# Three value projections join gate columns in pairs that use Strassen's products

## The chip, the cores and the metric

The kernel runs on one core of a Trainium2 chip. The metric is the device time of one execution in microseconds (us). Before the change it is 1405.8 us, the median of three runs from 1404.01 to 1406.87 us. The engines are named as in the profile: PE multiplies matrices, DVE and ACT work on whole tiles, POOL and SP here mostly issue transfers. Each engine runs its own list of instructions in a fixed order.

## The reference

One decoder layer on 256 tokens of width 2048, all in float32. Cut to what matters here:

```python
h = rmsnorm(x, g_mix)
proj = h @ w_in                                   # 2048 x (3*2048 + 3*2048)
q, k, v = first 3*2048 columns, 16 heads of 128 each
gates = sigmoid(the last 3*2048 columns)          # three branches
o_a = stick_breaking_attention(q[:4], k[:4], v[:4])
qn, kn = rmsnorm(q[4:]) * q_gain, rmsnorm(k[4:]) * k_gain
o_b, o_c = moba_attention(6 heads), dilated_attention(6 heads)   # softmax with biases
x = x + (sum over branches of gates * (o @ w_branch)) @ w_out
x = x + (silu(h2 @ w_g) * (h2 @ w_u)) @ w_down,   h2 = rmsnorm(x)
```

The change is in `proj` alone, 24 blocks of 512 columns: four each for q, k and v (a block is one group of four heads) and twelve for the gates (four column blocks of three branches).

## The kernel before, in words

**Precision.** Every float32 product is made of three: a weight tile (128 rows of K by two, 512 columns) is split by `split` (L110) into a high part, an ACT cast into `w_hi`, and a low part, a DVE subtraction into `w_lo`. `product` (L174 to L178) then does high by high, low by high, high by low, each a matmul of 128x512. `w_hi` and `w_lo` have five buffers each, so splits run at most five tiles ahead of PE.

**Plain blocks.** `project` multiplies one block of 512 columns over all of K: 8 splits and 16 x 2 x 3 = 96 matmuls (16 slices of K, two halves of the tokens).

**Pairs.** `project_pair` takes two blocks of columns at once. Half of K (chunks 0 and 1, `WC`) goes by Strassen's seven products: 7 x 2 x 2 x 3 = 84 matmuls in place of 96. The other half goes plainly: 96. A pair has 22 splits and 180 matmuls where two plain blocks have 16 and 192. It also forms sums of weight tiles on DVE (`add_into`, L320, six of 128x1024; L331 in `begin_pair`, two), copies three intermediate results on ACT (`snapshot`, L315) and combines results on DVE (L375, L377, L380, L389). In the order of the code, PE does: first product (weights b11), second (b21), fifth (sum `u`), two plain slices, sixth (`u`), a plain slice, seventh (`b12` + `b22`), a plain slice, third (b22), two plain slices, fourth (`u`), two plain slices. Each of these steps is twelve matmuls. ACT copies the first product right after it, and the fifth, sixth and seventh right after each of them.

**Stages.** Small generators run beside the projections. `parts` and `project` call `advance(stages)` at each split or slice and `advance(slow_stages)` at every second one. After a q and k pair of group g, `rows_to_columns` normalises and transposes q and k of that group: 16 sums of squares on ACT (L663, of 128x128), the root by Ln and Exp with two table loads (L185, L186) and eight small DVE steps (L189 to L192), a scaling on DVE for each of four tiles (L681), and then, for groups 0 to 2, transposes on PE (L198), copied out by DVE for q (L691) and by ACT for k (L688). Transposed tiles go through the PSUM pool `tr`, which has two buffers. For group 3 the transposes are made by DMA: ACT copies (L650), issues the transpose (L652), and eight splits later `join` copies the landed words (L673, ACT); q is then scaled on DVE (L676). `attention` of group g follows in `slow_stages` once `keep_v` has stored the values of the group, which needs the attention of the group before to be written out. Group 0 (stick-breaking) uses Ln and Exp on ACT and steps of 128x768 on DVE; groups 1 to 3 use softmax.

**Order.** A scheduler sets the order of instructions within an engine, except for those that `keep_in_program_order` pins. `add_into`, the DMA transposes and `join`'s copies are pinned. The order of the projection's units is the list `units`: v0, one gate block, qk0, qk1, v1, qk2, v2, qk3, v3, one gate block, and then five pairs of gate blocks. At the second of the five pairs the attention PSUM is given back, and the pairs use two further PSUM banks from then on (`beside`); before that all four banks of a pair come from `acc` (`in_turn`). From the same place the finished attention outputs are split for the next stage (`split_o`, four splits of 128x1024, one in each of the last four pairs).

Of the kernel before, what the change touches and what calls it, by code (L numbers as in the profile page):

```python
# [29 lines left out]
NB = 512  # L30
# [27 lines left out]
def hybrid_block(ctx: ExitStack, tc: tile.TileContext, x, w_in, w_branch, w_out, w_gu, w_down, rel_bias, xT, gains,  # L58
# [3 lines left out]
    w_in, w_branch, w_out, w_gu, w_down = (w[0] for w in (w_in, w_branch, w_out, w_gu, w_down))  # L62
# [20 lines left out]
    def pool(stack, name, side, bufs=1):  # L83
        return stack.enter_context(tc.tile_pool(name=name, bufs=bufs, side=side, reuse_waits="tile"))
# [8 lines left out]
    def half_kb(dt=F32):  # L93

        return scratch.tile([P, NB], dt, name="sc")
# [13 lines left out]
    def split(hi, lo, src, pin=False):  # L109
        for op in nc.scalar.copy(hi, src), nc.vector.tensor_sub(lo, src, hi.bitcast(F32)):  # L110
            if pin:
                tc.keep_in_program_order(op)
# [6 lines left out]
    split_count = [0]  # L119
    at_split = {}  # L120
# [31 lines left out]
    def finish_stages(queue):  # L152
        while queue:
            advance(queue)

    def project(acts, k0, w, row0, nk, col0, ps=None, done=0, last=1):


        ps = ps or banks()
        held = []  # L160
        for k, w_hi, w_lo in weights(w, row0, done, nk, col0):
            if k:
                advance(stages)
            if k % 2 == 0 and k:
                advance(slow_stages)
            held.append((k, w_hi, w_lo))
            if k < nk - last or k == nk - 1:
                for t in range(NT):
                    for kk, hi, lo in held:
                        product(ps[t], *acts.plain(t, k0 + kk), hi, lo, kk == 0, kk == nk - 1)  # L170
                held = []
        return ps
# [152 lines left out]
    def begin_pair(acts, w, colA, colB):  # L325

        b11, b12 = (quarter(acts, w, 0, col0) for col0 in (colA, colB))
        p11 = [parts(b) for b in b11]
        u = [gx.tile([P, 2, NB], F32, name="u") for _ in acts.wc]
        for a, b, d in zip(b11, b12, u):  # L330
            nc.vector.tensor_add(d, a, b)  # L331
        b21 = quarter(acts, w, 1, colA)
        return p11, b12, u, b21, [parts(b) for b in b21]
# [69 lines left out]
    hs = Both(p1, h, WC)  # L403
# [21 lines left out]
    V0 = 2 * NH * HD  # L425
# [43 lines left out]
    def first_norm():  # L469
        rows = []  # L470
        for c in range(4):
            rows.append(load_x(c, fetch))
            yield
            if c:
                squares(rows[c - 1], ss1, c - 1)
            yield
        squares(rows[3], ss1, 3)
        yield
        sst = small.tile([P, NT], F32, name="sst", bufs=1)
        nc.vector.tensor_reduce(sst, ss1, op=ALU.add, axis=AX.X)  # L480
        rsqrt_mean(rstd, sst, D, NT)
        yield
# [219 lines left out]
    def until_joined(g):  # L702
        while len(joined) < 4 * (g + 1):
            yield

    def attention(g, qT, kT, v):
        biases = []
        if g:
            for hl in (0, 2):
                bias = pa.tile([P, 2, S], F32, name="bias")  # L710
                nc.sync.dma_start(bias, bass.AP(tensor=vec.tensor, offset=vec.offset + (4 * g - H_A + hl) * NDIST,
                                                  ap=[[1, P], [NDIST, 2], [1, S]]))
                biases.append(bias)
        for hl in (0, 2):
            if g:
                yield from softmax_pair(4 * g + hl, hl, qT, kT, v, biases[hl // 2])
            else:
                yield from stick_breaking(hl, qT, kT, v)
            yield
# [3 lines left out]
    def keep_gate(c, b, srcs):  # L723
        for t in range(NT):
            gt = half_kb()
            nc.scalar.activation(gt, srcs[t], AF.Sigmoid, scale=rstd[:, t:t + 1])
            nc.gpsimd.dma_start(gate_mem[b, c, t], gt)
# [3 lines left out]
    def keep_v(g, ps):  # L731
        if g:
            finish_stages(slow_stages)
        heads["v", g] = v = pa.tile([P, NT, NB], F32, name="v", bufs=1)

        def scaled():
            for t in range(NT):
                nc.scalar.activation(v[:, t, :], ps[t], AF.Copy, scale=rstd[:, t:t + 1])
            yield

        if g:
            finish_stages([scaled()])
            slow_stages.append(until_joined(g))
            slow_stages.append(attention(g, *heads["qk", g], v))
        else:
            stages.extend((first_norm(), scaled()))

    def keep_qk(g, q0, q1, k0, k1):
        sbs = []
        if not g:  # L750
            q_scale = small.tile([P, NT], F32, name="sst", bufs=1)
            nc.vector.tensor_scalar(q_scale, rstd, SCALE, None, op0=ALU.mult)
        for t, (src, own) in enumerate(((q0, True), (q1, False), (k0, True), (k1, True))):
            sb = src if own else half_kb()
            nc.scalar.activation(sb, src, AF.Copy, scale=(rstd if g or t >= NT else q_scale)[:, t % NT:t % NT + 1])
            sbs.append(sb)
        heads["qk", g] = qkT = [pa.tile([P, 4, S], F32, name=f"{n}T") for n in "qk"]
        if g:
            stages.append(rows_to_columns(g, sbs, qkT))
        else:  # L760
            slow_stages.append(rows_to_columns(g, sbs, qkT))
            slow_stages.append(attention(g, *qkT, heads["v", g]))
# [1 line left out]


    chunks = [(c, b) for c in range(4) for b in range(3)]
    units = [("v", 0), ("gate", chunks[0]), ("qk", 0), ("qk", 1), ("v", 1), ("qk", 2), ("v", 2), ("qk", 3), ("v", 3)]
    units += [("gate", chunks[1])] + [("gates", chunks[i:i + 2]) for i in range(2, len(chunks), 2)]

    def gate_col(c, b):  # L770
        return 3 * NH * HD + b * D + c * NB

    def pair_of(kind, what):
        if kind == "qk":
            return hs, w_in, what * NB, NH * HD + what * NB
        if kind == "gates":
            return hs, w_in, gate_col(*what[0]), gate_col(*what[1])

    def in_turn():
        turn.reverse()  # L780
        return [acc.tile([P, NB], F32, name=turn[1]) for _ in range(2)]
# [4 lines left out]
    def split_o(k):  # L786
        split(o.hi[:, k:k + 4, :], o.lo[:, k:k + 4, :], o_raw[:, k:k + 4, :], True)
# [1 line left out]
    others = in_turn  # L789
    ahead = None  # L790
    for (kind, what), after in zip(units, units[1:] + [(None, None)]):
        if kind == "gates" and what[0] == chunks[4]:
            finish_stages(slow_stages)
            pat.close()
            acc2 = ctx.enter_context(tc.tile_pool(name="acc2", bufs=1, space=PSUM))
            others = beside
            o = Columns(pool(ph1, "o", "left"), "o", NH)
            for i in range(NH // 4):
                at_split[split_count[0] + 22 * i + 12] = [lambda k=4 * i: split_o(k)]
        nxt = pair_of(*after)  # L800
        if kind in ("qk", "gates"):
            ps, ahead = project_pair(*pair_of(kind, what), ahead, nxt)
            if others is in_turn:
                turn.reverse()
        else:
            ps = project(h, 0, w_in, 0, KT, V0 + what * NB if kind == "v" else gate_col(*what),
                         *((ps0, FIRST) if (kind, what) == ("v", 0) else ()))
            ahead = begin_pair(*nxt) if nxt else None
        finish_stages(stages)
        if kind == "v":  # L810
            keep_v(what, ps)
        elif kind == "qk":
            keep_qk(what, *ps)
        elif kind == "gate":
            keep_gate(*what, ps)
        else:
            keep_gate(*what[0], ps[:2])
            keep_gate(*what[1], ps[2:])
# [22 lines left out]
    for c in range(4):  # L841
        turning = [rooms[(NT * c + t) % len(rooms)] for t in range(NT)]
        ms = [room[:, :NB] for room in turning]
        for b, (k0, nk) in enumerate(((0, H_A), (H_A, H_B), (H_A + H_B, H_C))):
# [3 lines left out]
            ps = project(o, k0, w_branch, k0 * P, nk, c * NB)  # L848
# [49 lines left out]
    for c in range(4):  # L898
# [3 lines left out]
        ps = project(m, 0, w_out, 0, KT, c * NB)  # L902
# [250 lines left out]
```

## Time and profile before

| | |
|---|---|
| timed runs, median of 3 | 1405.8 us (1404.01 to 1406.87) |
| profiled execution, from first to last instruction | 1402.7 us |
| PE busy | 1394.4 us (99%) |
| DVE busy | 1208.7 us (86%) |
| ACT busy | 959.1 us (68%) |
| POOL busy | 20.1 us |
| HBM traffic over the span | 220 GB/s |
| granted PE clock, mean | 1.000 |

The profiled execution's own time is not listed beside its span; the median of the timed runs is 3.1 us longer than the span. A matmul record shows 0.39 us, but matmuls overlap: their starts stand about 0.2265 us apart, which is what one costs. In a list of groups the last numbers are busy time, the mean of one, and the idle time of the engine just before. In a table by stretch, the columns are us, then for each engine busy time and instructions in brackets, granted clock, DMA share and GB/s.

The stretches of the projection, read from where the results of each unit are taken: v0 and a gate block to 51 us, qk0 to 92, qk1 to 140, v1 to 170, qk2 to 213, v2 to 246, qk3 to 286, v3 to 313, a gate block to 331, and the pairs of gate blocks to 378, 420, 461, 502 and 544 us.

### The profile page before, as it was taken

What the parts mean: (1) busy time and instruction counts of PE and PEld (TensorE: products, weight loads), DVE (VectorE), ACT (ScalarE), POOL (GpSimd) and SP (SyncE); (2) the same over time, 40 slices, a digit from 0 to 9 for tenths busy, and PEclk for the clock granted to TensorE, in tenths of its full rate; (3) what the DMA queues carried; (4) which work ended last, traced back from release to release, by engine and by line L of the source; (5) the groups of instructions that cost most, each with busy time, mean ns of one, the idle gap of its engine ahead of it and who ended that gap; (6) DMA issues with size and microseconds to landing.
All of it is one profiled execution on the core that took longest, in us unless ns stands there. A gap on an engine that the chain in (4) does not pass through costs nothing. (4 is left out here: it accounts for less than half of the span.)

```text
span 1402.7 us, 17407 instructions
## 1 busy us (share of the span) xinstructions
PE 1394.4 (99%) x6197; PEld 1150.2 (82%) x6197; DVE 1208.7 (86%) x1290; ACT 959.1 (68%) x1204; POOL 20.1 (1%) x45
## 2 busy tenths in 40 slices
PE   9999999999999999999999999999999999999998
PEld 7888888888888888888878888888888888788887
DVE  6997887857899997875789999999999998997887
ACT  7777867787767675666767677776776776754553
POOL 1000000000000000000000000000000000000000
PEclk9999999999999999999999999999999999999999
DMA  9764647684657667998876766677877779877562
GB/s 341 277 225 125 235 123 251 182 228 137 235 202 246 223 200 264 326 278 243 263 232 239 225 205 222 205 210 250 250 234 240 231 226 307 281 239 260 196 198 87
DMA packets 208967, 320.56 MB, mean 229 GB/s; under 512 B 53064, under 2 KB 65376, under 8 KB 208880
## 3 DMA queue, kind: packets, MB, share of 16 engines
q1 hardware_dynamic: 153216, 293.64, 62.8%
q10 hardware_dynamic: 53136, 17.86, 6.6%
q0 software_dynamic: 2528, 7.95, 1.5%
q8 instruction: 48, 0.79, 0.2%
q14 instruction: 39, 0.32, 0.1%
HBM read 294.22 MB, written 14.70 MB: 220 GB/s over the span
## 5 line engine op out<-in xcount | busy, mean ns | idle before, releaser
L110 DVE TENSOR_TENSOR w_lo<-w_raw,w_hi 128x1024 fp32r<-128x1024 f32 x324 | 393.0, 1220 | 96.9 <-ACT w_hi L110 95.3
L110 ACT CAST w_hi<-w_raw 128x1024 fp32r<-128x1024 f32 x324 | 337.2, 1050 | 107.1 <-PE qs L178 29.5
L110 ACT CAST w_hi<-g_raw 128x1024 fp32r<-128x1024 f32 x192 | 199.8, 1052 | 110.4 <-PE ps L178 38.1
L110 ACT CAST w_hi<-u 128x1024 fp32r<-128x1024 f32 x144 | 151.5, 1053 | 150.2 <-DVE u L320 75.5
L110 DVE TENSOR_TENSOR w_lo<-g_raw,w_hi 128x1024 fp32r<-128x1024 f32 x192 | 228.8, 1220 | 25.4 <-ACT w_hi L110 24.3
L110 DVE TENSOR_TENSOR w_lo<-u,w_hi 128x1024 fp32r<-128x1024 f32 x144 | 172.2, 1220 | 19.0 <-ACT w_hi L110 13.7
L177 PE MATMUL ps<-w_lo,h_hi 128*128 128x512 f32 x352 | 137.5, 391 | 0.0
L178 PE MATMUL ps<-w_hi,h_lo 128*128 128x512 f32 x352 | 137.3, 390 | 0.0
L176 PE MATMUL ps<-w_hi,h_hi 128*128 128x512 f32 x352 | 131.2, 390 | 0.0
L177 PE MATMUL qs<-w_lo,h_hi 128*128 128x512 f32 x332 | 129.8, 391 | 0.0
L178 PE MATMUL qs<-w_hi,h_lo 128*128 128x512 f32 x332 | 129.3, 390 | 0.0
L176 PE MATMUL qs<-w_hi,h_hi 128*128 128x512 f32 x332 | 124.6, 394 | 0.0
L320 DVE TENSOR_TENSOR u<-u,g_raw 128x1024 f32<-128x1024 f32 x80 | 94.4, 1219 | 0.0
L177 PEld LDWEIGHTS ps<-w_lo,h_hi 128*128 128x128 f32 x352 | 66.1, 188 | 13.8
L178 PEld LDWEIGHTS ps<-w_hi,h_lo 128*128 128x128 f32 x352 | 66.1, 188 | 13.6
L176 PEld LDWEIGHTS ps<-w_hi,h_hi 128*128 128x128 f32 x352 | 65.9, 188 | 13.6
L178 PEld LDWEIGHTS qs<-w_hi,h_lo 128*128 128x128 f32 x332 | 62.3, 188 | 13.0
L176 PEld LDWEIGHTS qs<-w_hi,h_hi 128*128 128x128 f32 x332 | 62.3, 188 | 12.8 <-issue 0.2
L177 PEld LDWEIGHTS qs<-w_lo,h_hi 128*128 128x128 f32 x332 | 62.4, 188 | 12.7
L331 DVE TENSOR_TENSOR u<-g_raw 128x1024 f32<-128x1024 f32 x40 | 48.7, 1219 | 10.7 <-DMA g_raw<-in_w_in 9.5
L320 DVE TENSOR_TENSOR g_raw<-g_raw 128x1024 f32<-128x1024 f32 x40 | 47.1, 1218 | 0.0
L177 PE MATMUL v<-w_lo,h_hi 128*128 128x512 f32 x120 | 46.9, 390 | 0.0
(400 smaller groups left out, 2933.1 us busy)
## 6 DMA issues: line engine op xcount, KB each, us to landing
w_raw<-in_w_in SPq DMA_DIRECT2D x116, 512.0 KB, 4.8
g_raw<-in_w_gu SPq DMA_DIRECT2D x88, 512.0 KB, 5.5
w_raw<-in_w_gu SPq DMA_DIRECT2D x88, 512.0 KB, 5.9
g_raw<-in_w_in SPq DMA_DIRECT2D x72, 512.0 KB, 5.7
w_raw<-in_w_down SPq DMA_DIRECT2D x56, 512.0 KB, 5.3
w_raw<-in_w_branch SPq DMA_DIRECT2D x32, 512.0 KB, 5.9
w_raw<-in_w_out SPq DMA_DIRECT2D x32, 512.0 KB, 4.7
g_raw<-in_w_down SPq DMA_DIRECT2D x32, 512.0 KB, 5.3
```

The source lines that it names most:

```text
L110: for op in nc.scalar.copy(hi, src), nc.vector.tensor_sub(lo, src, hi.bitcast(F32)):
L176: nc.tensor.matmul(ps, ah, wh, start=start, stop=False, **how)
L177: nc.tensor.matmul(ps, ah, wl, start=False, stop=False, **how)
L178: nc.tensor.matmul(ps, al, wh, start=False, stop=stop, **how)
L320: tc.keep_in_program_order(nc.vector.tensor_add(d, d, a))
L331: nc.vector.tensor_add(d, a, b)
```

## The change

The plain blocks v1, v2, v3 and the second gate block, and one of the pairs of gate blocks, are regrouped: each of v1, v2, v3 is now made in a pair with one gate block (`vg`). The units become v0, a gate block, qk0, qk1, vg1, qk2, vg2, qk3, vg3, and four pairs of gate blocks. Of 24 blocks, 22 are now in eleven pairs (18 in nine before). The first results of a `vg` pair go to `keep_v`, the second to `keep_gate`. The attention PSUM is now given back at the last but one pair of gates (`LAST_HEADS = 2`), so attention 3 has two pairs of gates to run beside, and `split_o` is called every eleven splits in the last two pairs and at the start of the next stage.

```diff
-    units = [("v", 0), ("gate", chunks[0]), ("qk", 0), ("qk", 1), ("v", 1), ("qk", 2), ("v", 2), ("qk", 3), ("v", 3)]
-    units += [("gate", chunks[1])] + [("gates", chunks[i:i + 2]) for i in range(2, len(chunks), 2)]
+    units = [("v", 0), ("gate", chunks[0]), ("qk", 0), ("qk", 1)]
+    for g in range(1, 4):
+        units += [("qk", g)] * (g > 1) + [("vg", (g, chunks[g]))]
+    units += [("gates", chunks[i:i + 2]) for i in range(4, len(chunks), 2)]
+    LAST_HEADS = 2
...
+        if kind == "vg":
+            return hs, w_in, V0 + what[0] * NB, gate_col(*what[1])
...
-        if kind == "gates" and what[0] == chunks[4]:
+        if kind == "gates" and what[0] == chunks[4 + 2 * LAST_HEADS]:
...
-                at_split[split_count[0] + 22 * i + 12] = [lambda k=4 * i: split_o(k)]
+                at_split[split_count[0] + 11 * i + 8] = [lambda k=4 * i: split_o(k)]
...
-        if kind in ("qk", "gates"):
+        if kind in ("qk", "gates", "vg"):
             ps, ahead = project_pair(*pair_of(kind, what), ahead, nxt)
...
+        elif kind == "vg":
+            keep_v(what[0], ps[:2])
+            keep_gate(*what[1], ps[2:])
```

The scheduler makes a new order of it. Three places matter below; in each, rows of the same step stand before and after. The first is DVE while q and k of group 2 are normalised, beside v2 before:

```order
L192 TENSOR_TENSOR rr<-rs_y_2003,rs_t_2006 128x16
L110 TENSOR_TENSOR w_lo<-g_raw,w_hi 128x1024
L681 TENSOR_TENSOR sc<-sc,rr 128x512 x4
L110 TENSOR_TENSOR w_lo<-g_raw,w_hi 128x1024
L110 TENSOR_TENSOR w_lo<-u,w_hi 128x1024
L691 TENSOR_TENSOR qT<-tr,gq 128x4x128
L110 TENSOR_TENSOR w_lo<-u,w_hi 128x1024
```

The same step beside vg2, on DVE in the changed kernel:

```order
L192 TENSOR_TENSOR rr<-rs_y_2272,rs_t_2275 128x16
L681 TENSOR_TENSOR sc<-sc,rr 128x512 x2
L320 TENSOR_TENSOR g_raw<-g_raw 128x1024 x2
L681 TENSOR_TENSOR sc<-sc,rr 128x512 x2
L691 TENSOR_TENSOR qT<-tr,gq 128x4x128 x2
L110 TENSOR_TENSOR w_lo<-g_raw,w_hi 128x1024 x2
```

The sums for the seventh product (L320 into `g_raw`) and its low parts (the last row) now stand between and behind the six steps of the normalisation.

The second place is DVE at group 3, beside v3 before:

```order
L192 TENSOR_TENSOR rr<-rs_y_2630,rs_t_2633 128x16
L681 TENSOR_TENSOR sc<-sc,rr 128x512 x4
L110 TENSOR_TENSOR w_lo<-w_raw,w_hi 128x1024 x2
L676 TENSOR_TENSOR qT<-qT,gq 128x4x128
L110 TENSOR_TENSOR w_lo<-w_raw,w_hi 128x1024 x2
```

And beside vg3 in the changed kernel:

```order
L192 TENSOR_TENSOR rr<-rs_y_3088,rs_t_3091 128x16
L681 TENSOR_TENSOR sc<-sc,rr 128x512 x4
L375 TENSOR_TENSOR sc<-sc 128x512
L377 TENSOR_TENSOR sc<-qs,sc 128x512
L380 TENSOR_TENSOR sc<-qs,sc 128x512
L676 TENSOR_TENSOR qT<-qT,gq 128x4x128
L320 TENSOR_TENSOR u<-u,g_raw 128x1024 x2
L110 TENSOR_TENSOR w_lo<-u,w_hi 128x1024 x2
L331 TENSOR_TENSOR u<-g_raw 128x1024 x2
L110 TENSOR_TENSOR w_lo<-w_raw,w_hi 128x1024
```

Before, two splits stood ready between the scaling of the rows and L676, which needs the transposed words. Now the sums for the fourth product (L320 into `u`) stand behind L676.

The third place is ACT at the same step of group 3 in the changed kernel:

```order
L650 COPY sc<-sc 128x1024
L315 COPY sc<-ps 128x512
L650 COPY sc<-sc 128x1024
L652 DMA_TRANSPOSE sc<-sc 128x8x128
L650 COPY sc<-sc 128x1024
L652 DMA_TRANSPOSE sc<-sc 128x8x128 x2
L673 COPY qT<-sc 128x2x4x128
L110 CAST w_hi<-u 128x1024 x2
L650 COPY sc<-sc 128x1024
L110 CAST w_hi<-w_raw 128x1024
```

Before, a cast of `w_raw` stood between the last L650 and the first L673. Now no cast stands between the first L650 and L673, and the casts for the fourth product come behind it.

## The prediction

> **What bounds the kernel now.** I read the page's totals first, then a table of busy times by stretch over the units that change, and then the records of ACT and DVE behind each q and k pair.
>
> ```profile
> span 1402.7 us, 17407 instructions
> PE 1394.4 (99%) x6197; PEld 1150.2 (82%) x6197; DVE 1208.7 (86%) x1290; ACT 959.1 (68%) x1204; POOL 20.1 (1%) x45
> ```
>
> PE is busy for 99% of the span, so a matmul that is taken away is time saved, unless PE then waits for its weights. Whether it can wait is read from the stretches: v2, v3, the first pair of gates with an attention beside it, and a pair of gates alone.
>
> ```profile
> 212.80:246.00 33.20, 32.96 (x162) 27.50 (x161) 25.46 (x35) 24.79 (x57) 0.00 (x0) 1.00 0.73 245
> 286.30:313.00 26.70, 26.70 (x121) 22.14 (x120) 15.24 (x24) 23.30 (x54) 0.00 (x0) 1.00 0.79 206
> 331.00:378.00 47.00, 47.00 (x221) 39.13 (x220) 40.66 (x50) 32.78 (x52) 1.08 (x2) 1.00 0.51 177
> 420.50:461.30 40.80, 40.80 (x181) 33.78 (x181) 38.00 (x37) 27.55 (x32) 2.16 (x4) 1.00 0.69 231
> ```
>
> A pair of gates takes 40.8 us for 180 matmuls, 0.2265 us each, and DVE is busy for 38.0 of it. The plain units v2 and v3 leave DVE idle for 7.7 us of 33.2 and 11.5 us of 26.7. It is in these loose units that the normalisation of the group just projected runs, and the change replaces them by pairs.
>
> **The gain.** One plain pair of blocks costs 192 matmuls, a Strassen pair 180. Two more pairs take away 24 matmuls of 128x512: 24 x 0.2265 = 5.4 us. No transfer is added, and the order of the work from the next stage on is as before.
>
> **The cost in DVE work.** The two more pairs bring 12 splits, 12 and 4 sums of L320 and L331, and 8 combinations.
>
> ```profile
> 446.39 2.36 DVE L320 TENSOR_TENSOR u<-u,g_raw 128x1024 f32<-128x1024 f32 x2
> 448.66 0.68 DVE L377 TENSOR_TENSOR sc<-v,sc 128x512 f32<-128x512 f32 x1
> ...
> 456.67 4.62 DVE L110 TENSOR_TENSOR w_lo<-g_raw,w_hi 128x1024 fp32r<-128x1024 f32 x4
> 461.21 0.68 DVE L389 TENSOR_TENSOR sc<-ps,sc 128x512 f32<-128x512 f32 x1
> ```
>
> Starts stand 1.13 us apart (2.27 / 2, 4.54 / 4) for the large ones and 0.6 for the small, so 28 x 1.13 + 8 x 0.6 = 36.5 us, which the idle DVE time of the old plain units (v2 and v3 alone 19) and that of the pairs would nearly take up. So the sum over the region is not the bound. The question is the order: in a `vg` pair the sums and low parts of the late products stand, on the same in-order engine, behind steps of the normalisation, which themselves wait for ACT. A stop comes where that chain is longer than the work that PE has ahead. I follow the chain at each place, with these rows.
>
> ```profile
> 214.94 0.31 ACT L663 ACTIVATE sc<-sc 128x128 f32<-128x128 f32 x1
> ...
> 219.65 2.93 ACT L110 CAST w_hi<-w_raw 128x1024 fp32r<-128x1024 f32 x3
> 222.59 1.28 ACT L185 ACT_TABLE_LOAD   x1
> 223.88 0.22 ACT L185 ACTIVATE rs_y<-rs_v 128x16 f32<-128x16 f32 x1
> 224.12 1.28 ACT L186 ACT_TABLE_LOAD   x1
> 225.41 0.21 ACT L186 ACTIVATE rs_y<-rs_y 128x16 f32<-128x16 f32 x1
> 225.53 1.99 ACT L110 CAST w_hi<-g_raw 128x1024 fp32r<-128x1024 f32 x2
> ```
>
> Sixteen squares take 219.65 - 214.94 = 4.71 us, 0.294 each; three casts 2.94, 0.98 each; the two loads with Ln and Exp 225.53 - 222.59 = 2.94.
>
> ```profile
> L315 ACT COPY sc<-qs x35: 565/579/590, 59.4 to 1150.2; 128x512 f32<-128x512 f32 x35
> L557 ACT ACTIVATE p<-p x2: 848/848/848, 116.5 to 142.1; 128x768 f32<-128x768 f32 x2
> ```
>
> ```profile
> 300.16 0.17 DVE L189 TENSOR_TENSOR rs_t<-rs_y 128x16 f32<-128x16 f32 x1 [0.30 <-ACT rs_y L186]
> ...
> 301.30 1.22 DVE L110 TENSOR_TENSOR w_lo<-w_raw,w_hi 128x1024 fp32r<-128x1024 f32 x1
> ...
> 302.85 2.50 DVE L681 TENSOR_TENSOR sc<-sc,rr 128x512 f32<-128x512 f32 x4
> ```
>
> The eight small steps take 302.85 - 300.16 less the split between, 1.56 us; a scaling L681 takes 2.50 / 4, and 0.60 by the overlap of neighbours that the smaller rows above show.
>
> [...]
>
> **vg2.** From the end of PE's fifth product, ACT copies it (0.58), does 8 squares (2.35), 3 casts (2.93), both loads with Ln and Exp (2.94): 8.8. DVE: eight small steps 10.4, two scalings 11.6, two sums L320 13.8, two scalings 15.0, one L691 15.6.
>
> ```profile
> 237.29 0.68 DVE L691 TENSOR_TENSOR qT<-tr,gq 128x512 f32<-128x512 f32 x1
> 237.90 1.22 DVE L110 TENSOR_TENSOR w_lo<-u,w_hi 128x1024 fp32r<-128x1024 f32 x1
> ```
>
> The second L691 needs PE's next four transposes, and PE makes them once the first has freed a buffer of `tr`: 0.5, then 0.6, and the first low part for the seventh product follows at 17.9. PE has four steps to do until then, 48 x 0.2265 = 10.9, and about 2.7 us of transposes and attention, 13.7 in all.
>
> ```profile
> 240.56 1.03 PE L198 MATMUL tr<-ident,sc 128*128 128x128 f32 x8
> 121.97 1.02 PE L569 MATMUL att<-pT,neg_after 128*128 128x512 f32 x2
> 136.00 0.59 PE L583 MATMUL tr<-p,v 128*128 128x256 f32 x2
> ```
>
> So PE stops for about 4.2 us. Bounds: 3.5 if some squares run before the copy, 5 if the transposes come late. I take 4.2, since each link has its own row. Behind the waiting L691 on DVE stand the low parts, and for these PE waits.
>
> **vg1** carries both the normalisation of group 1 and the stick-breaking steps, whose rows on DVE are these.
>
> ```profile
> 127.33 0.95 DVE L574 TENSOR_TENSOR p<-p,att 128x768 f32<-128x768 f32 x1
> ...
> 132.73 0.76 DVE L577 TENSOR_TENSOR p<-p,before 128x256 f32<-128x256 f32 x2
> ```
>
> From the end of the first product: copy, cast, 5 squares, load and Ln (0.85) 5.15; two DVE steps of 0.95 and the masks, 7.9; a low part and two sums, 11.3; L574, 12.2; three low parts 15.6; masks and small steps 18.0; four scalings, two sums, two L691, 23.8; the low part of the seventh 25.0. PE has six steps, 16.3, with 1.7 of L569 to L573, 1.3 of L583 and L584, 16 transposes (2 x 1.03 less overlaps, 1.7) and 0.7 of other small ones: 21.7. Stop 3.3, and 1.5 to 5, since some of these twenty links wait for nothing and may slide forward.
>
> **vg3.** Here the turned words come by DMA, and `add_into` of the fourth product stands behind L676.
>
> ```profile
> 303.57 1.99 ACT L650 COPY sc<-sc 128x1024 uint16<-128x1024 uint16 x2 [0.47 <-DVE sc L681]
> ...
> 310.24 1.37 ACT L673 COPY qT<-sc 128x1024 uint16<-128x1024 uint16 x1
> ```
>
> ```profile
> L652 ACTq DMA_TRANSPOSE sc<-sc x4: 1247/1333/2407, 304.6 to 309.8; - x4
> ...
> DMA to landing us min/median/max: 3.5/5.5/6.6
> ```
>
> ```profile
> 310.37 1.23 DVE L110 TENSOR_TENSOR w_lo<-w_raw,w_hi 128x1024 fp32r<-128x1024 f32 x1 [3.89 <-ACT w_hi L110]
> 311.64 0.69 DVE L676 TENSOR_TENSOR qT<-qT,gq 128x512 f32<-128x512 f32 x1
> ```
>
> From the end of the first product: copies, squares, five casts and the loads, 15.2; seven low parts and small steps, 24.5; a scaling 25.1; L650 26.1; a snapshot 26.7; issue to landing 5.5, 32.2; L673 33.6; L676 34.3; two sums 36.5; the first low part 37.7. PE comes to the fourth product after eleven steps of 2.72, 29.9, with small ones 30.1: it stops for 7.6. Then low part, two L331 and low part take 4.5 against 2.9 of PE: 1.6 more. In all 9.2; with landings of 3.5 and 6.6 it is 7.2 to 10.3. Before, the same wait cost nothing: DVE idled 3.89 us there, with splits already ahead of it. Now ACT's casts of the fourth product's sums are queued behind the waiting L673, and DVE's sums behind the waiting L676; what covered it, splits made ahead, stands behind them.
>
> **Small.** Two `split_o` of a pair now run in each of the last two: 0.3 (0 to 1).
>
> **The sum.** -5.4 + 3.3 + 4.2 + 9.2 + 0.3 = +11.6, so a span of 1402.7 + 11.6 = 1414.3. The profiled execution's span is 3.1 us under the median of the timed runs, 1405.8; with the same difference the time is 1417.4, and I say **1417**. The low ends give -5.4 + 1.5 + 3.5 + 7.2 = +6.8, 1412.6; the high ones -5.4 + 5 + 5 + 10.3 + 1 = +15.9, 1421.7.
>
> **The rivals.**
>
> *The gain is kept* (faster). The scheduler's order makes room: ACT's squares start early, DVE's idle time shifts, five tiles of weights bridge each wait. For it: the pair at 331 carried attention with PE at 47.00 of 47.00, and v2 swallowed a wait of DVE for a transfer with PE at 32.96 of 33.20:
>
> ```profile
> 222.14 1.23 DVE L331 TENSOR_TENSOR u<-g_raw 128x1024 f32<-128x1024 f32 x1 [7.17 <-DMA g_raw<-in_w_in]
> ```
>
> Against it: neither carried a normalisation and a pair. It holds if each chain begins earlier than I have it by as much as its stop, 3.3, 4.2 and 9.2 us. Time: 1405.8 - 5.4 = 1400.4.
>
> *Half the stops.* Only vg3's DMA chain is real, at its lower 5 to 6 us, and vg1 and vg2 are hidden: -5.4 + 6 = about 1406, no change.
>
> *PE's clock falls.* PE's longest wait after its first matmul is 0.64 us, and at the start of the program matmuls come slower:
>
> ```profile
> 1.52 3.35 PE L396 MATMUL tr<-sc 128*128 128x512 f32 x7 [1.52 <-DVE sc L407]
> ...
> 7.51 0.74 PE L459 MATMUL ps<-w_hi,h_hi 128*128 128x512 f32 x2
> ...
> 1224.33 0.50 PE L176 MATMUL tr<-w_hi,a_shi 128*128 128x512 f32 x1 [0.64 <-ACT w_hi L110]
> ```
>
> From 1.52 to 7.51 they are 13 in 5.99 us, where 13 x 0.2265 = 2.94. If the 7.6 us in vg3 brings that back, 3.0 us more: 1420. [...]
>
> **Chances.** Forecast 0.53, range of its own 1412 to 1422; clock 0.15; half the stops 0.13; gain kept 0.17; 0.02 for anything else. A measurement tells 0.2%, 2.8 us, from no change. Faster is the gain kept and a fifth of the half case, 0.20; same 0.12; slower 0.68. The range leaves out the gain kept (0.17) and little else: from the low end of half the stops, 1403, to 1424, the high end of the forecast with most of the slow clock, which would be 3.0 more.
>
> **What would show it.** In the profile after: PE idle before the seventh product of vg1 and vg2, released by `w_lo`, of 3 to 4 us each; about 7 us before the fourth product in vg3, with L676 just ahead of L320 on DVE and L673 waiting for a transfer; 24 fewer matmuls. If PE is busy throughout 140 to 331 us, the chains were wrong and time is saved; if the granted clock falls below 1 near 290 us, the third rival holds.

## The result, and the profile after

The changed kernel takes 1420.84 us, the median of four runs (1417.55 to 1423.25), where the kernel before takes 1406.34 us beside it. The ratio is 1.011, with a 95% interval of 1.0091 to 1.0129: 14.5 us slower. The forecast was 1417, range 1403 to 1424.

The page of the changed kernel, its totals:

```profile
span 1421.5 us, 17432 instructions
PE 1400.5 (99%) x6173; PEld 1150.3 (81%) x6173; DVE 1243.1 (87%) x1326; ACT 978.6 (69%) x1228; POOL 20.1 (1%) x45
```

PE has 6173 matmuls, 24 fewer than before, and DVE has 36 more instructions, as the change says. This profiled execution was the slowest of the four (1423.25 us), and its span is 18.8 us longer than the one before. 2.6 us of that lie in the next stage, at 609 and 666 us, where matmuls waited 1.40 and 1.21 us for ACT's casts of `m`; most of the profiles below don't have these waits. Three of the executions below, whose mean granted clock was 0.65 or 0.85, are left out of the times.

The table by stretch, one row per unit that matters: vg1, vg2 and vg3 of the changed kernel. After the time come, for each engine, busy us and instructions, then the granted clock.

```profile
140.90:197.50 56.60, 52.92 (x229) 42.36 (x228) 48.94 (x65) 39.83 (x81) 0.00 (x0) 0.94 0.47 156
241.10:292.40 51.30, 48.42 (x214) 39.29 (x213) 42.58 (x51) 35.63 (x71) 0.00 (x0) 0.93 0.54 185
339.30:388.10 48.80, 43.99 (x180) 35.19 (x180) 41.79 (x49) 40.45 (x72) 0.00 (x0) 0.93 0.69 180
```

Two losses stand in each row. PE does nothing for 56.60 - 52.92 = 3.7, 2.9 and 4.8 us, 11.4 in all. And the clock is 0.93 to 0.94 where it was 1.00 in every stretch before: 0.06 x 52.9 + 0.07 x 48.4 + 0.07 x 44.0 = 9.6 us, give or take 0.7 from the rounding. With the 24 matmuls saved, -5.4 + 11.4 + 9.6 = +15.6; with the 2.6 of the next stage that is 18.2 of the 18.8 by which this profile is longer.

The median is only 14.5 longer, and the clock differs from run to run: its mean over the span is 0.992, 0.994, 0.995 and 0.996 in the four runs, from the slowest to the fastest. That is 11.4, 8.5, 7.1 and 5.7 us of their spans, each give or take 0.7, so the 5.7 us between the slowest run and the fastest can be the clock's alone.

Where PE stops, in the records of PE (start, duration, and in brackets the wait just before and what ended it). First vg1:

```profile
152.44 0.98 PE L176 MATMUL qs<-w_hi,h_hi 128*128 128x512 f32 x2 [2.26 <-ACT w_hi L110]
```

ACT's records at that place:

```profile
146.84 0.33 ACT L663 ACTIVATE sc<-sc 128x128 f32<-128x128 f32 x1
...
148.44 1.28 ACT L557 ACT_TABLE_LOAD   x1
149.73 0.84 ACT L557 ACTIVATE p<-p 128x768 f32<-128x768 f32 x1
...
151.36 1.03 ACT L110 CAST w_hi<-w_raw 128x1024 fp32r<-128x1024 f32 x1
```

From 146.84 to 151.36 ACT does five squares, a table load with Ln (of group 0's attention), and three more squares; the cast that PE wants stands behind them. PE stands in the plain slices behind the fifth product, well ahead of the seventh, where I had looked for the stop. The other 1.4 us of vg1 come there, in three waits from 167.91 to 170.25 us, the longest of them 0.89 for DVE's L691.

In vg2, DVE and then PE:

```profile
258.98 1.29 DVE L681 TENSOR_TENSOR sc<-sc,rr 128x512 f32<-128x512 f32 x2
260.19 2.35 DVE L320 TENSOR_TENSOR g_raw<-g_raw 128x1024 f32<-128x1024 f32 x2
262.46 1.29 DVE L681 TENSOR_TENSOR sc<-sc,rr 128x512 f32<-128x512 f32 x2
263.66 1.28 DVE L691 TENSOR_TENSOR qT<-tr,gq 128x512 f32<-128x512 f32 x2
```

```profile
259.82 0.63 PE L198 MATMUL tr<-ident,sc 128*128 128x128 f32 x4 [0.54 <-DVE sc L681]
...
261.34 0.66 PE L198 MATMUL tr<-ident,sc 128*128 128x128 f32 x4 [0.57 <-ACT pT L621]
262.54 0.64 PE L176 MATMUL ps<-w_hi,b_shi 128*128 128x512 f32 x1 [0.55 <-ACT w_hi L110]
264.40 1.11 PE L198 MATMUL tr<-ident,sc 128*128 128x128 f32 x4 [1.22 <-DVE qT L691]
```

This is the forecast chain, root, scalings, sums, scalings, L691. PE is held four times in five microseconds, by the scaled rows, by ACT's copy of the attention's transposes (L621), by the cast of the sum, and by the buffer of `tr` that L691 frees, 2.9 us together where I had one stop of 4.2.

In vg3, ACT, DVE and PE:

```profile
371.74 1.33 ACT L673 COPY qT<-sc 128x1024 uint16<-128x1024 uint16 x1 [1.70 <-DMA sc<-sc]
375.03 2.18 ACT L110 CAST w_hi<-u 128x1024 fp32r<-128x1024 f32 x2 [1.95 <-DVE u L320]
```

```profile
373.11 0.69 DVE L676 TENSOR_TENSOR qT<-qT,gq 128x512 f32<-128x512 f32 x1 [2.80 <-ACT qT L673]
373.72 2.35 DVE L320 TENSOR_TENSOR u<-u,g_raw 128x1024 f32<-128x1024 f32 x2
```

```profile
376.12 0.80 PE L176 MATMUL ps<-w_hi,h_hi 128*128 128x512 f32 x1 [3.97 <-ACT w_hi L110]
...
378.40 0.63 PE L176 MATMUL ps<-w_hi,h_hi 128*128 128x512 f32 x1
378.83 0.63 PE L177 MATMUL ps<-w_lo,h_hi 128*128 128x512 f32 x1
```

The fourth product waits 3.97 us, through the sums, L676 and L673, for a transfer, exactly the queue of the forecast. Behind it matmuls start 0.43 us apart (378.40 to 378.83) in place of 0.2265: the slow clock.

Read in steps of 0.2 us, the granted clock is 1.00 or 0.50, with the values between only in steps in which it changes. It falls four times: twice in vg1, from 153.5 and from 170.6 us on, for 3.41 us each, and once each in vg2 (from 262.8) and vg3 (from 375.4), for 6.83 us. At 0.50 matmuls start 0.43 us apart for 0.2265, so about half of such a time is lost, an estimated 1.7 or 3.4 us, or less where PE stands anyhow. A stretch of the first three (the last stands further below, with its own experiment):

```profile
154.00:156.00 2.00, 2.00 (x6) 1.54 (x5) 2.00 (x3) 1.69 (x10) 0.00 (x0) 0.50 0.24 25
172.00:174.00 2.00, 2.00 (x8) 1.71 (x7) 2.00 (x2) 1.56 (x3) 0.00 (x0) 0.50 0.03 8
264.00:266.00 2.00, 1.59 (x6) 1.47 (x7) 2.00 (x4) 2.00 (x3) 0.00 (x0) 0.50 0.00 0
```

### The profile page after: what moved, and what is told of

Its sections match the earlier page's. It is cut to its first block, busy times and chain, and to the rows that moved or that the text cites. A ratio compares the mean times of both kernels' runs of the same rounds, so it can differ in the third digit from the quotient of the medians.

```text
span 1421.5 us, 17432 instructions
## 1 busy us (share of the span) xinstructions
PE 1400.5 (99%) x6173; PEld 1150.3 (81%) x6173; DVE 1243.1 (87%) x1326; ACT 978.6 (69%) x1228; POOL 20.1 (1%) x45
## 5 line engine op out<-in xcount | busy, mean ns | idle before, releaser
L110 DVE TENSOR_TENSOR w_lo<-w_raw,w_hi 128x1024 fp32r<-128x1024 f32 x308 | 374.4, 1223 | 81.5 <-ACT w_hi L110 80.2
L110 ACT CAST w_hi<-w_raw 128x1024 fp32r<-128x1024 f32 x308 | 320.2, 1050 | 88.9 <-DMA w_raw<-in_w_branch 28.3
L110 ACT CAST w_hi<-g_raw 128x1024 fp32r<-128x1024 f32 x208 | 215.8, 1051 | 99.6 <-DVE g_raw L320 30.4
L110 ACT CAST w_hi<-u 128x1024 fp32r<-128x1024 f32 x156 | 164.0, 1053 | 156.5 <-DVE u L320 82.8
L110 DVE TENSOR_TENSOR w_lo<-g_raw,w_hi 128x1024 fp32r<-128x1024 f32 x208 | 247.7, 1224 | 20.7 <-ACT w_hi L110 19.8
L110 DVE TENSOR_TENSOR w_lo<-u,w_hi 128x1024 fp32r<-128x1024 f32 x156 | 187.0, 1224 | 29.8 <-ACT w_hi L110 28.5
L178 PE MATMUL ps<-w_hi,h_lo 128*128 128x512 f32 x328 | 128.6, 392 | 0.0
L176 PE MATMUL ps<-w_hi,h_hi 128*128 128x512 f32 x328 | 122.5, 395 | 4.0 <-ACT w_hi L110 4.0
L320 DVE TENSOR_TENSOR u<-u,g_raw 128x1024 f32<-128x1024 f32 x88 | 103.9, 1221 | 0.0
L320 DVE TENSOR_TENSOR g_raw<-g_raw 128x1024 f32<-128x1024 f32 x44 | 51.8, 1220 | 0.0
L176 PE MATMUL v<-w_hi,h_hi 128*128 128x512 f32 x104 | 40.6, 391 | 0.0
```

The costliest lines, as they stand in the source:

```text
L176: nc.tensor.matmul(ps, ah, wh, start=start, stop=False, **how)
L178: nc.tensor.matmul(ps, al, wh, start=False, stop=stop, **how)
L320: tc.keep_in_program_order(nc.vector.tensor_add(d, d, a))
```

## The experiments

The theory: in a pair, the steps of the normalisation stand on ACT and DVE among the casts, sums and low parts of the late products; the chain is longer than what PE has ahead, PE stops, and its clock then falls. Rivals: the later `split_o`; the pairs themselves, normalisation or not; the weights' transfers.

### One pair at a time, and the later splits alone

Three kernels pair one of v1, v2, v3 with a gate block and leave the other two plain. The edit for v1:

```diff
-    for g in range(1, 4):
-        units += [("qk", g)] * (g > 1) + [("vg", (g, chunks[g]))]
-    units += [("gates", chunks[i:i + 2]) for i in range(4, len(chunks), 2)]
+    for g in range(1, 4):
+        units += [("qk", g)] * (g > 1) + [("vg", (g, chunks[1])) if g == 1 else ("v", g)]
+    units += [("gates", chunks[i:i + 2]) for i in range(2, len(chunks), 2)]
```

> The change with v1 alone in a pair with a gate block; v2, v3 plain again, five pairs of gates behind. One pair more than before: 12 matmuls fewer, -2.7 us. Theory (each pair with a normalisation beside it stops PE on its own, and PE runs slowly after): the changed kernel's profile shows in vg1 2.26 and 1.42 us without PE work and 3.3 us by a granted clock of 0.77 to 0.94, 7.0 together, so +4.3 us against before, about 1410.6. Rival 1 (the loss comes from the attention outputs split later, which this kernel also has): -2.7 and +2.5 of the next stage, about 1406. Rival 2 (the three pairs disturb each other, no loss with one alone): 1403.6.

> The change with v2 alone in a pair. Theory: -2.7 + 2.9 us without PE work + 2.7 of slow clock as in the changed kernel = +2.9, about 1409.2. Rival 1 (outputs split later): about 1406. Rival 2 (no loss alone): 1403.6.

> The change with v3 alone in a pair. Theory: -2.7 + 4.8 us without PE work + 2.6 of slow clock = +4.7, about 1411. Rival 1 (outputs split later): about 1406. Rival 2 (no loss alone): 1403.6.

And the kernel before with the later `split_o` alone:

```diff
-        if kind == "gates" and what[0] == chunks[4]:
+        if kind == "gates" and what[0] == chunks[8]:
...
-                at_split[split_count[0] + 22 * i + 12] = [lambda k=4 * i: split_o(k)]
+                at_split[split_count[0] + 11 * i + 8] = [lambda k=4 * i: split_o(k)]
```

> The kernel before with nothing but the attention outputs split later (all four in the last two pairs of gates). Theory: no difference, 1406.3 within 1 us. Rival 1: the next stage's first matmuls wait for ACT's casts as in the profile of the changed kernel (1.5 and 1.4 us at 609 and 666 us), +2.5 us, about 1409.

The kernel before took 1404.54 us beside these four. The later splits alone: 1405.55 us, ratio 1.0007 (0.9995 to 1.0019), no clear difference. That rival falls as the cause of 14.5 us, though a cost of up to 2.7 us is not excluded: the profile, of the slowest of its ten runs (1413.07 us), has the wait for `m` again, 2.7 us at the longest, and a mean granted clock of 0.998 where the kernel before has 1.000. With one pair alone: 1415.45 (1.0082, 1.0067 to 1.0097) for vg1, 1410.77 (1.0057, 1.0036 to 1.0077) for vg2, 1410.20 (1.0041, 1.0026 to 1.0056) for vg3. Each pair costs time on its own, and its stops are those of the changed kernel to within 0.2 us: 2.25 us for the cast with vg1 alone, and with vg3 alone

```profile
324.62 0.80 PE L176 MATMUL ps<-w_hi,h_hi 128*128 128x512 f32 x1 [4.04 <-ACT w_hi L110]
```

But the three sums (+10.9, +6.2, +5.7, where I had +4.3, +2.9 and +4.7) are not the pairs' prices. In the first two kernels v3 is followed at once by a pair of gates, where before a plain gate block stood, and the end of group 3's normalisation now runs beside that pair. It makes stops of its own there. PE with vg2 alone:

```profile
338.58 0.50 PE L176 MATMUL ps<-w_hi,b_shi 128*128 128x512 f32 x1 [1.18 <-ACT v L738]
...
341.79 0.49 PE L176 MATMUL ps<-w_hi,b_shi 128*128 128x512 f32 x1 [1.57 <-ACT w_hi L110]
```

So the experiment changed two things, which I had not seen ahead. It says the same of the mechanism (a pair beside a normalisation stops PE wherever they meet), and only vg3's +5.7 comes near to a price by itself.

### The normalisation left out

Squares, root and scaling are removed from the changed kernel.

```diff
-            ss = pa.tile([P, 4 * NT * 2], F32, name="ss", bufs=1)
...
-                    nc.scalar.activation(junk[:, cols], sb[:, cols], AF.Square,
-                                         accum_out=ss[:, 4 * i + hd:4 * i + hd + 1])
...
-            rr = pa.tile([P, 4 * NT * 2], F32, name="rr", bufs=1)
-            rsqrt_mean(rr, ss, HD, 4 * NT * 2)
...
-                nc.vector.tensor_mul(sb3, sb3, rr[:, 4 * i:4 * i + 4, None].to_broadcast([P, 4, HD]))
```

> The changed kernel without the normalisation of q and k in groups 1 to 3 (squares, root and scaling are left out; the transposes stay). Theory (the stops come from the normalisation's steps on ACT and DVE, which stand ahead of the late products' casts, sums and low parts): PE is busy through all three pairs with one gate, the gain of 5.4 us shows, about 1400 to 1401. Rival (the pairs of v and a gate are bound by DVE's work or by their weight transfers, normalisation or not): at least half of the loss stays, 1410 or more.

It took 1434.32 us (1.0217, 1.0198 to 1.0236), which was neither. The stretch from 900 to 1100 us, far behind the edit and dense with matmuls, shows where the time went, in this kernel and then in the next one:

```profile
900.00:1100.00 200.00, 200.00 (x862) 162.15 (x861) 186.44 (x176) 145.86 (x158) 0.00 (x0) 1.00 0.73 224
```

```profile
900.00:1100.00 200.00, 200.00 (x884) 165.66 (x883) 189.90 (x180) 147.82 (x160) 0.00 (x0) 1.00 0.77 233
```

862 matmuls where the kernel before and the next one do 884, at a granted clock of 1.00. In the first pair too they start 0.2323 us apart (59.78 to 62.80 us), for 0.2271 in the next kernel (59.78 to 62.96). With the root went its small tiles, and in the built program the addresses behind them moved by 384 bytes. The activations `h`, which start at a multiple of 512 bytes in the kernel before, the changed one and the next, started 128 bytes behind one. The next kernel leaves the same work out and keeps the tiles:

```diff
+            for n in "vyt":
+                small.tile([P, 4 * NT * 2], F32, name=f"rs_{n}16")
+            for n in ("ss", "rr"):
+                pa.tile([P, 4 * NT * 2], F32, name=n, bufs=1)
```

> As the run without normalisation in groups 1 to 3 (squares, root and scaling left out), but with the small tiles of the root still allocated, so that the activations lie at multiples of 512 bytes again (there they had moved to 128 bytes behind one, and every matmul of the program, the first ones too, took 0.2324 us in place of 0.2267). Theory (the stops come from the normalisation's steps): matmuls 0.2267 us apart and two or three waits of about 1 us left, as in that run's profile, 1400 to 1403. Rival (bound by the pairs themselves): 1410 or more.

1404.73 us beside 1404.54 for the kernel before, ratio 1.0008 (0.9998 to 1.0018). So of the 14.5 us lost and the 5.4 that had been hoped for on top, leaving out the normalisation gives back some 14. The three pairs in this kernel:

```profile
140.40:192.10 51.70, 49.98 (x230) 40.37 (x229) 44.99 (x53) 34.91 (x48) 0.00 (x0) 1.00 0.50 170
235.40:280.50 45.10, 45.10 (x213) 37.52 (x212) 38.62 (x37) 28.58 (x34) 0.00 (x0) 1.00 0.62 210
327.80:371.00 43.20, 41.85 (x184) 34.04 (x184) 38.41 (x37) 33.45 (x37) 0.00 (x0) 1.00 0.78 221
```

The clock is back at 1.00 and PE stops for 1.7, 0 and 1.4 us in place of 3.7, 2.9 and 4.8. The rival of the pairs as such falls for the greater part, and with it that of the weights' transfers, which this kernel makes too. The first does not fall altogether: 3.1 us of stops stay. The 2.3 us that should then be left of the 5.4 are not seen in the median; the profiled execution, its fastest, has 1.6 of them (a span of 1401.1 us against 1402.7), and where they are in the others stays open.

### Which half of the chain

Two kernels were meant to leave out the squares alone (the sums are set to one by POOL), and the root and the scaling alone (their lines as in the first diff above).

```diff
...
-                    nc.scalar.activation(junk[:, cols], sb[:, cols], AF.Square,
-                                         accum_out=ss[:, 4 * i + hd:4 * i + hd + 1])
+                if not i:
+                    nc.gpsimd.memset(ss, 1.0)
```

> The changed kernel without the sums of squares of groups 1 to 3 (48 squares on ACT, 14.1 us of its time, are left out, their sums set to one; root and scaling stay). Leaving all of the normalisation out took 15.4 us off the changed kernel. Theory A (ACT's squares hold up the casts): 9 us or more of it come back, 1411 or less. Theory B (the chain of table loads, small steps and scaling does it, as the waits in vg2 and vg3 read): only the stop of 2.3 us in vg1 and its slow clock go, and the chain in vg2 and vg3 starts some 2 us earlier, 4 to 7 us in all, 1414 to 1417.

> The changed kernel with the squares, but without the root (table loads, Ln, Exp and eight small steps) and without the scaling of the rows in groups 1 to 3; tiles stay allocated. Theory B: the stops in vg2 and vg3 go with their slow clock, 9 us or more, 1411 or less, and vg1 keeps its stop of 2.3 us before a cast. Theory A: 6 us at most, 1415 or more.

The first kernel leaves more out of the pairs than I meant. Where the sums are constants the root waits for nothing, and the scheduler put the Ln and Exp of all three roots at the start of the program. ACT, the first and the last of them:

```profile
7.69 0.20 ACT L185 ACTIVATE rs_y<-rs_v 128x16 f32<-128x16 f32 x1
...
17.22 0.21 ACT L186 ACTIVATE rs_y<-rs_y 128x16 f32<-128x16 f32 x1
```

So neither squares nor roots stand in these pairs, but for the last small step of two roots on DVE. The roots' four table loads in vg2 and vg3 are gone too, and half of the scalings run before the pairs. The time is 1402.68 us, 0.9981 of the kernel before (0.9970 to 0.9992), with stops of 0.1, 0.7 and 1.1 us. It says much what the run without normalisation said, and it does not test Theory A, although it came out at A's forecast. Why leaving out the scaling too is 2 us slower (1404.73) I don't know; the scheduler makes a different order of each.

Without root and scaling, the squares in place: 1409.78 us, 1.0032 (1.0021 to 1.0044), 5.0 us above the kernel before. Some 9.5 us of the 14.5 have come back, where Theory B had 9 or more and A at most 6. The three pairs:

```profile
140.60:195.20 54.60, 50.80 (x223) 40.29 (x223) 44.07 (x47) 39.41 (x80) 0.00 (x0) 0.97 0.47 155
239.00:285.20 46.20, 46.20 (x219) 38.36 (x218) 40.19 (x40) 34.38 (x74) 0.00 (x0) 1.00 0.57 188
331.60:376.50 44.90, 42.40 (x183) 33.80 (x182) 38.21 (x36) 37.55 (x69) 0.00 (x0) 1.00 0.70 210
```

vg1 is in the main a matter of the squares on ACT: without the root it still stops for 3.8 us, 2.3 of them before the same cast, at a clock of 0.97. In vg2 the squares by themselves stop nothing, so the root and the scaling are needed for its stops, and vg3 loses half of its 4.8. The 4.8 us that come back when the squares go too are near what vg1 loses there to that one stop and the slow clock, 2.3 + 1.5 (0.03 x 50.8 us). How much the squares delay the root behind them in vg2 and vg3 no run separates.

### Four attempts to mend it

Copies of the transposed words later, so that the fourth product's sums come ahead of L676:

```diff
-            behind(split_count[0] + (8 if g else 6), join, dst[j][:, :, t * P:(t + 1) * P], turned, j)
+            behind(split_count[0] + (14 if g else 6), join, dst[j][:, :, t * P:(t + 1) * P], turned, j)
```

> The changed kernel with the copies of the transposed words of group 3 (L673, and the scaling L676 behind them) fourteen splits after their transfer's issue in place of eight, so that the fourth product's sums stand ahead of them. Theory: DVE starts these sums 3.4 us earlier, PE's stop of 4.1 us falls to under 1 and the slow clock behind it goes: 6 us less than the changed kernel, about 1415. Rival (DVE and ACT are late there anyhow): 2 us less at most.

1418.58 us (1.0112, 1.0087 to 1.0136), by the ratio the time of the changed kernel. The fourth product's sums did come first, and the stop of vg3 shrank from 3.97 us to two of 0.69 and 0.93, but others appeared at the next pair, the longest of 0.93 at 390.00 us. In vg3:

```profile
367.31 0.50 PE L176 MATMUL ps<-w_hi,h_hi 128*128 128x512 f32 x1 [0.69 <-ACT w_hi L110]
368.74 0.50 PE L176 MATMUL ps<-w_hi,h_hi 128*128 128x512 f32 x1 [0.93 <-ACT sc L315]
```

The normalisation's steps further apart:

```diff
                                          accum_out=ss[:, 4 * i + hd:4 * i + hd + 1])
                 yield
+                yield
...
             rsqrt_mean(rr, ss, HD, 4 * NT * 2)
             yield
+            yield
+            yield
```

> The changed kernel with the normalisation's steps further apart: two splits for each tile's squares in place of one, two more between the root and the scaling. The root and scaling then stand behind the seventh product's sums in vg1 and vg2. Theory: the stop of 2.3 us in vg1 (ACT's squares in one stretch) and those of 2.9 us in vg2 go, with their slow clock, 8 to 11 us less than the changed kernel, about 1411; vg3 keeps its wait. Rival (the chain only moves, and PE stops at the third or fourth product): the same time within 3 us.

1424.74 us (1.015, 1.0126 to 1.0175), slower than the changed kernel by 4 us, or by 6 by the ratios. PE now waits at the end of vg3 and behind it, for DVE to empty its PSUM bank and for ACT to copy one:

```profile
392.77 0.47 PE L176 MATMUL ps<-w_hi,h_hi 128*128 128x512 f32 x1 [4.44 <-DVE sc L389]
...
399.76 0.51 PE L176 MATMUL qs<-w_hi,b_shi 128*128 128x512 f32 x1 [2.41 <-ACT sc L315]
```

The rival was right that the chain only moves, if not in the time, which it had within 3 us.

Root and scalings on POOL:

```diff
-            rsqrt_mean(rr, ss, HD, 4 * NT * 2)
+            rsqrt_mean(rr, ss, HD, 4 * NT * 2, nc.gpsimd)
...
-                nc.vector.tensor_mul(sb3, sb3, rr[:, 4 * i:4 * i + 4, None].to_broadcast([P, 4, HD]))
+                nc.gpsimd.tensor_mul(sb3, sb3, rr[:, 4 * i:4 * i + 4, None].to_broadcast([P, 4, HD]))
```

> The changed kernel with the small steps of the root (L183, L189 to L192), the scaling L681 and the scaling L676 of group 3 on POOL, which is idle, in place of DVE. Theory (DVE's steps that wait for ACT or a transfer hold up the sums and low parts queued behind them): DVE no longer waits there, the stop of 4.1 us in vg3 and those of vg2 go in the main with their slow clock, about 8 to 11 us less than the changed kernel, 1410 to 1413. Rival (the chain itself is late, whoever does it, since PE's own transposes wait for it): as the changed kernel, 1418 or more; slower, if POOL needs over 2 us for a scaling.

1421.50 us (1.0118, 1.0103 to 1.0133): again no gain. ACT's records in vg3:

```profile
360.87 1.04 ACT L650 COPY sc<-sc 128x1024 uint16<-128x1024 uint16 x1 [3.48 <-POOL sc L681]
```

DVE no longer waits for the root, but ACT stands 3.48 us before L650 with the casts queued behind it. My theory in its narrow form, that it is DVE's waiting steps that do it, is not borne out: here another in-order queue that feeds PE, ACT's, waits for the late step. But POOL also takes longer over the chain, 9.0 us from the root's first small step to the last scaling (354.81 to 363.83) where the same steps by themselves take DVE some 4.1 (1.56 + 2.50), so what an idle engine as fast as DVE would give is not shown.

Matmuls that nobody reads ahead of the fourth product of vg3 (16, kept in their place, as are now that product and the slices before it):

```diff
...
         add_into(u, b21)
+        if pad:
+            fill(pad)
         form(X, 4, u, False, False)
```

> The changed kernel with 16 matmuls of 128x512 whose result nobody reads ahead of the fourth product of vg3, where PE waits 4.1 us. Theory (an idle PE loses its clock): they fill 3.6 us of the wait, the matmuls behind it run at 0.23 us again in place of 0.43, and the 2.6 us of slow clock in vg3 are saved, 1418 where the changed kernel has 1420.8. Rival (the slow matmuls behind a stop have another cause): the same 1421, clock as before.

1420.72 us (1.0117, 1.0086 to 1.0148), the median of runs from 1416.52 to 1424.05: no clear gain in time. On the clock it is clear, though. The same stretch in this kernel, from ahead of the fill to well behind the fourth product's first matmuls:

```profile
370.00:376.00 6.00, 6.00 (x28) 4.93 (x27) 5.31 (x6) 3.97 (x5) 0.00 (x0) 1.00 0.44 129
376.00:384.00 8.00, 6.78 (x30) 5.26 (x29) 8.00 (x9) 7.94 (x9) 0.00 (x0) 1.00 1.03 235
```

And in the changed kernel:

```profile
371.00:378.00 7.00, 2.56 (x9) 1.42 (x8) 4.86 (x5) 4.22 (x4) 0.00 (x0) 0.81 0.54 132
378.00:384.00 6.00, 6.00 (x19) 4.75 (x18) 6.00 (x7) 6.00 (x7) 0.00 (x0) 0.65 1.17 271
```

With PE kept busy the clock stays at 1.00 (0.81 and 0.65 without). The slow clock of vg3 is thus a consequence of the stop. vg3 as a whole took no less: from DVE's last step of the pair before to its last step of vg3 48.75 us, as against 48.78 in the changed kernel. The 16 matmuls take 3.6 us themselves, and stops of 1.40 us ahead of the fill and 1.22 in the plain slices behind the fourth product have come in. This profile is of the slowest of the four runs, and 6.0 us of its span are waits in the next stages (662 and 738 us), which have nothing to do with the fill as far as the rows show.

No version that does all the work and beats both kernels was found. The run in which neither squares nor roots stood in the pairs was 2 us ahead of the kernel before; a way to have both done ahead of the pairs was not tried.

## Why the prediction was right, and where not

**The gain**: right. 24 matmuls fewer.

**The direction and the cause**: right. The normalisation's chain in the pairs stops PE; without the normalisation the loss is gone (1404.73 us), and the late splits cost nothing that is clear of the noise (1.0007), as the small term of 0.3 (0 to 1) said.

**vg1**, 3.3 us: the size is near (3.7), the place is not. I followed DVE's low parts to the seventh product; the larger stop, 2.26 us, came earlier, in the plain slices, for a cast on ACT behind eight squares and a table load. I had five of the squares and the load in the sum and went on from there to DVE; the three squares and the cast behind them were not in it, and I did not compare them with PE's arrival. The chain that I followed was about as long as I had it, 26.5 us from the first product to the end of the seventh's first low part (145.4 to 171.9) for 25.0; PE was late itself by then, and waited only 1.4 there. That the sizes agree is luck.

**vg2**, 4.2 us: the chain is the one described, link by link, and about as long: the first low part of the seventh product was done 17.7 us after the fifth product (248.4 to 266.1) for 17.9. It cost 2.9. PE had more to do meanwhile than the 13.7 us in my sum, part of it at a granted clock of 0.50 (from 262.8 us on).

**vg3**, 9.2 us: the mechanism was right, and it is the term most mis-sized, 4.8. Three steps of it were too long. I let the fourth product wait for both sums and a low part (37.7 us after the first product), but its first matmul needs only the cast of the first sum, and it started at 376.12, 33.7 us after the first product's end at 342.4. The first transfer was issued 25.2 us after that end (367.62), not at 26.7, behind the snapshot, and it took 4.1 us from there to L673, not 5.5.

**The slow clock**: this is the step that failed. I gave it as a rival at 3.0 us for one stop of over 7 us in vg3. It came at all three pairs, in four falls, 9.6 us together in the profiled run, and the sum had nothing for it. For vg3 the price was about right (0.07 x 44.0 = 3.1), and the condition was wrong: 2.26 us without a matmul in vg1 sufficed, and so did four short waits of 2.9 us together in vg2. They did not always: with the later copies the stop of vg1 was again 2.26 us and the clock behind it 1.00 (152 to 160 us), and in 30 us of the kernel with vg1 alone (320 to 350 us) 2.9 us of waits passed at 1.00.

So stops of 11.4 where I had 16.7, and a slow clock of 9.6 where I had none: two errors of opposite sign, which left the sum, +11.6 forecast against +14.5, closer than its terms. That is luck. 1420.8 lies in the range, and near the clock rival's time of 1420, but by four falls of the clock and smaller stops.

**The table loads**: the two loads with Ln and Exp took 2.94 us in vg2 (254.24 to 257.18), as in the rows before, with Ln (from 255.53 us) right behind its load of 1.28 us.

**The rivals on the other side**: the gain kept and half the stops had 0.30 between them and did not come.

## What to carry to other kernels

Idle time of the helping engines is not waste where a chain of dependent small steps runs beside the dense work: the plain units looked loose (DVE idle 7.7 of 33.2 us in v2), and it was this looseness that let the squares, the root and the scaling pass without holding up a cast. Before filling such a unit, follow the chain on every in-order queue that feeds the bound engine, and compare each queue's next delivery with PE's arrival, not just the last. And give stops of PE of the sizes met here (2.26 us in one piece, 2.9 us in four waits) a chance of a slow clock behind them, here nothing, 1.7 or 3.4 us a time, where 5.4 us in all were to be won. Where an input is made constant to leave a step out, look in the new trace for what else has moved.

## What the runs showed of the hardware that I had not expected

A shift of addresses slowed the matmuls. The two kernels without the normalisation differ only in five small tiles that are allocated and not used. Without these tiles, and with the activations 128 bytes behind a multiple of 512, 862 matmuls fitted into 200 us in place of 884, 0.2320 us each for 0.2262, at a granted clock of 1.00 in both. The whole program was 30 us longer for it (1434.32 against 1404.73 us). That it is the activations' address, and not another of the tiles that moved with them, was not separated.

PE's clock fell at short stops, but not at every stop. In the profile of the changed kernel it fell to 0.50, twice for 3.41 us and twice for 6.83. Its mean over the span is 0.992 to 0.998 in ten profiles (this one the lowest), and 0.999, 1.000 and 0.999 in those of the three kernels without the squares. The stop in vg1 before the cast, some 2.3 us, is in six profiles. Behind it the clock fell in the changed kernel (0.50 from 153.5 us on) and with vg1 alone (matmuls start 0.43 us apart, 155.70 to 156.13), and without the root vg1 ran at 0.97. With the later copies the clock stayed at 1.00:

```profile
151.96 0.98 PE L176 MATMUL qs<-w_hi,h_hi 128*128 128x512 f32 x2 [2.26 <-ACT w_hi L110]
```

```profile
152.00:160.00 8.00, 8.00 (x34) 6.13 (x35) 8.00 (x11) 7.57 (x23) 0.00 (x0) 1.00 0.21 66
```

Stops of 3.97 us (the changed kernel, 0.50 from 375.4 us on, still within the stop) and of 4.44 us (the normalisation's steps further apart, matmuls behind it 0.43 us apart from 393.72 to 396.28) came with a fall. Waits of 1.18, 1.57 and 0.76 us within 6 us (vg2 alone, the last until 343.05) had none up to 344 us: matmuls start 0.23 to 0.24 us apart, 343.39 to 343.86. What decides between these was not found. With 16 matmuls that nobody reads in place of the stop of vg3, the clock there was 1.00 from 370 to 384 us.

A scaling of 128x512 (L681) takes 1.04 us on POOL, the median of twelve, where DVE needs 0.63 (2.50 for four).
